# A two-way state scan without its identity matmul: the decayed state copied by ScalarE and added by VectorE, with some steps beside the scan in other places

## The chip, the cores and the metric

The kernel runs on one core of a Trainium2 chip. The metric is the device time of one execution in microseconds. A core has five engines that each work through a queue of their own in order: TensorE (PE in the profile; its weight loads stand apart as PEld), VectorE (DVE), ScalarE (ACT), GpSimd (POOL) and SyncE (SP), which here only issues transfers. They meet at semaphores. An instruction that waits holds up all that stands behind it in its queue.

## What is computed

The reference is a trunk of four layers over 512 latent and 256 context tokens of 1024 channels: a convolution layer, a bidirectional linear-attention layer (RWKV-7), an attention layer and another convolution layer. Only the second one's recurrence matters here. For each of 16 heads of 64 channels, and each of two directions, a 64 x 64 state S is carried over 768 tokens:

```python
def step(S, inp):
    d_t, k_t, v_t, kk_t, a_t = inp[:5]
    sa = jnp.einsum("bhvk,bhk->bhv", S, -kk_t)
    S = (S * d_t[:, :, None, :] + sa[..., None] * (kk_t * a_t)[:, :, None, :]
         + v_t[..., None] * k_t[:, :, None, :])
    out = jnp.einsum("bhvk,bhk->bhv", S, inp[5]) if emit else None
    return S, out
```

## The kernel before

**Tiling.** The recurrence is worked in chunks of 64 tokens, 12 chunks to a sequence. Two heads make a pair that fills the 128 partitions: head 0 on partitions 0 to 63 (`A` in the code), head 1 on 64 to 127 (`B`). There are eight pairs, 0 to 7, and `scan(p, d, G)` carries pair `p` in direction `d` (0 forward, 1 backward) through steps i = 0 to 11. Both directions of a pair are interleaved; the pairs follow each other.

**A step** has six parts, each ended by a `yield`. A tile `VT` holds, for head 0, the state S on rows A and the chunk's values on rows B, and for head 1 the other way round.

1. c: TensorE multiplies `VT` by a triangular matrix `GM` (L1346). For 0 < i < 11 it also multiplies `VT` by a slice of the identity (L1350), which puts S itself into `pS`, as the first term of a sum that is left open.
2. Z: ScalarE copies c from PSUM (L1353).
3. TensorE multiplies S by `AR` into the output `pO` (L1357), and Z by `Tt`, the inverse of a triangular matrix (L1360).
4. U: ScalarE copies the result into `VT` in place of S (L1362, L1363, four copies of 64 x 64 for both directions).
5. TensorE adds the chunk's terms to `pO` (L1366) and `BKT` times `VT` to `pS` (L1369), which closes both sums.
6. S: ScalarE writes the next step's state, `pS` times the chunk's decay `dc`, a scale for each partition (L1374, two copies of 64 x 64 a direction). The output goes from `pO` to the tile `O`, by a ScalarE copy for i in 0, 1, 4, 5, 6, 7 (L1379) and by a VectorE sum in the others (L1381).

`pO` and `pS` are two halves of one PSUM tile `o0` or `o1`.

**What runs beside it.** While pair p is scanned, the same queues prepare later pairs. `feats` makes decays and scaled keys of a quarter (half a sequence of one direction, four to a pair) of a later pair, in eleven steps: step 2 loads and multiplies (L1112, `pz`), step 3 is a tanh on ScalarE (L1116), step 4 a VectorE scaling (L1118, `sg`), step 5 the matmul that sums up decays (L1122, `pc`), step 6 an exponential (L1126, `Dt`), and then GpSimd's products (L1137 to L1144). `grams` builds `GM` and `BKT`. `inverse` computes the 32 x 32 triangular inverses of pair p + 1 in 31 steps of a product and a sum, nearly all on VectorE (L1265, L1268). `values` transposes v on TensorE (L1227) into one PSUM buffer and copies it into `VT`, rows B by VectorE and then rows A by ScalarE (both through `cpy`, L1089 and L1091), four times for half a sequence. `centre` takes the mean off pair p - 1's output and forms its variance.

**What sets the order.** The four compute engines run in the order in which the code records them; there is no scheduler there. A turn of a pair is 72 ticks; the scan does two parts of one direction in a tick, the even ones direction 0 and the odd ones direction 1. After every odd tick those side steps are recorded whose due time lies in the two ticks. The due times are numbers in `OPT`: `D` for the first six steps of `feats` and `F` for the rest (four rows, for the four quarters of a pair, 18 ticks to a quarter), `G` for `grams`, `I` for the inverse, `V0` and `V1` for the nine steps of `values` for the two half sequences. A pair's scan begins at tick 4, so three slots of two ticks repeat: parts 1 and 2 at ticks that leave 4 or 5 when divided by 6 (Z slot), parts 3 and 4 at 0 or 1 (U slot), parts 5 and 6 at 2 or 3 (S slot).

Of the kernel before, what the change touches and what calls it, by code (L numbers as in the profile page):

```python
# [8 lines left out]
F32 = mybir.dt.float32  # L9
F32R = mybir.dt.float32r  # L10
AF = mybir.ActivationFunctionType
ALU = mybir.AluOpType
# [3 lines left out]

D = 1024
P = 128
NT = D // P
CTX = 256  # L20
# [13 lines left out]
    G=[[1.1, 3.6, 4.6, 6.6, 9.6, 11.6, 13.1, 14.6, 17.9], [0.5, 3.1, 5.1, 7.6, 10.6, 11.6, 12.6, 14.6, 17.1], [1.6, 3.6,  # L34
        5.1, 5.1, 8.1, 12.1, 12.1, 14.1, 15.6], [1.6, 3.6, 5.1, 7.6, 9.6, 11.6, 13.1, 15.1, 16.6]],
    F=[[2.65, 6.65, 10.65, 15.65, 16.65], [3.65, 7.15, 9.65, 17.4, 17.9], [3.15, 7.15, 10.65, 16.15, 17.9], [1.65, 7.15, 10.65, 15.65, 17.9]],
    D=[[8.2, 13.7, 13.7, 14.2, 17.4, 17.9], [5.7, 12.7, 14.2, 16.9, 17.9, 17.9], [9.2, 12.7, 13.2, 13.7, 16.7, 17.7],
        [8.2, 13.7, 14.2, 14.7, 17.7, 17.9]],
    L=0.85,
    I=[3.9, 7.5, 8.4, 8.5, 9.75, 9.75, 9.75, 9.9, 11.9, 12.25, 13.5, 13.75, 13.9, 15.25, 15.4, 15.75, 17, 17.15, 17.65,  # L40
# [3 lines left out]
    V0=[31.91, 36.16, 37.91, 39.91, 40.91, 42.41, 43.66, 45.41, 46.91],  # L44
    V1=[47.92, 51.4375, 52.96, 54.43, 55.4275, 57.16, 58.42, 60.415, 62.1869],
    A=[64.18, 65.3143, 66.1364, 69.4498, 69.7397, 70.3889],
    B=[2.44, 4.09473, 7.27024, 8.71365, 9.3943, 9.83957],
    C=[12.2, 14, 16.1, 16.15, 18.75, 20.8, 21.45, 22.9, 23.55, 26.6, 28.95, 29.25, 32.1, 33.4, 36.55, 37.75],
# [30 lines left out]
class Trunk:  # L79
# [111 lines left out]
    def modulation(self, i, w=512):  # L191
# [3 lines left out]
        b = self.vbase[f"mod_b{i}"]  # L195
        half, nq = D // 2 // w, w // P
        order = [x * 2 * half + y for h in range(2) for x in (0, 1) for y in range(h * half, h * half + half)]
# [93 lines left out]
    def conv_layer(self, i, j, lat_only, filler):  # L291
# [27 lines left out]
        parts = {"a": 0, "b": 1, "g": 2}  # L319
        cols = [w_in[:, parts[x] * D + m * P: parts[x] * D + (m + 1) * P] for x, m in order if x != "c"]  # L320
        with tc.tile_pool(name="cv", bufs=1) as cv, tc.tile_pool(name="cd", bufs=1, space=DRAM) as cd:
# [340 lines left out]
    def rwkv_features(self, i, c1, cv):  # L662
# [103 lines left out]
        def modulation(i, w=256):  # L766

            modT, b = self.modT[i], self.vbase[f"mod_b{i}"]
            half, nq = D // 2 // w, w // P
            order = [x * 2 * half + y for h in range(2) for x in (0, 1) for y in range(h * half, h * half + half)]  # L770
# [257 lines left out]
    def rwkv_scan(self, i, rk, cv, vproj):  # L1028
        nc, tc, I = self.nc, self.tc, self.I
        C = 64  # L1030
# [9 lines left out]
        late = {}  # L1040
# [18 lines left out]
        ident = self.ident  # L1059
        self.mask3 = self.mask.rearrange("p (g c) -> p g c", c=C).unsqueeze(1).to_broadcast([P, 3, 2, C])  # L1060
        A, B = slice(0, 64), slice(64, 128)
# [24 lines left out]
        def cpy(key, k, out, in_):  # L1086
            e = OPT["E"][key][k]
            if e == "a":
                nc.scalar.activation(out, in_, AF.Copy)  # L1089
            elif e == "d":  # L1090
                nc.vector.tensor_copy(out, in_)  # L1091
            else:
                nc.gpsimd.tensor_scalar(out=out, in0=in_, scalar1=1.0, scalar2=0.0, op0=ALU.mult, op1=ALU.add)
# [235 lines left out]
        def scan(p, d, G):  # L1329


            if d == 0:
                G["O"] = late["s"].tile([P, TOK], F32, tag="O", name="O", bufs=2)
            O, Tt = G["O"], G["Tt"]
            for i in range(12):
                h, q = divmod(i, NQ)
                assert (p, h) in vdone and (p, h, d) in gdone and (p, h) in idone
                VT, GM, AR, BKT = (G["VT", h], *(G[n, h, d] for n in ("GM", "AR", "BKT")))
                dc = G["DC", h, d][:, q:q + 1]
                hc = lambda hd: slice(hd * C, (hd + 1) * C)  # L1340
                pc = late["c"][d][:, 0:2 * C].rearrange("p (n c) -> p n c", c=C)
                po = late["p"].tile([P, 2 * C], F32, tag=f"o{d}", name=f"o{d}")
                pO, pS = po[:, 0:C], po[:, C:]
                for hd, own, oth in ((0, A, B), (1, B, A)):
                    rows = oth if i == 0 else slice(0, P)
                    nc.tensor.matmul(pc[own, 0, :], GM[rows, 2 * hd, q, :], VT[rows, d, q, hc(hd)], start=True, stop=True)  # L1346

                if 0 < i < 11:
                    for hd, own in ((0, A), (1, B)):
                        nc.tensor.matmul(pS[own], ident[:, hc(hd)], VT[:, d, q, hc(hd)], start=True, stop=False)  # L1350
                yield
                Z = late["s"].tile([P, C], F32, tag=f"Z{d}", name="Z", bufs=1)
                cpy("Z", d, Z, pc[:, 0, :])  # L1353
                yield
                if i:
                    for hd, own in ((0, A), (1, B)):
                        nc.tensor.matmul(pO[own], VT[own, d, q, hc(hd)], AR[own, 1, q, :], start=i == 11, stop=False)  # L1357
                tu = (h * 2 + d) * NQ + q
                for own in (A, B):
                    nc.tensor.matmul(pc[own, 1, :], Tt[own, tu, :], Z[own], start=True, stop=True)  # L1360
                yield
                cpy("U", 2 * d, VT[A, d, q, 0:C], pc[A, 1, :])  # L1362
                cpy("U", 2 * d + 1, VT[B, d, q, C:2 * C], pc[B, 1, :])  # L1363
                yield
                for hd, own in ((0, A), (1, B)):
                    nc.tensor.matmul(pO[own], VT[:, d, q, hc(hd)], GM[:, 2 * hd + 1, q, :], start=i == 0, stop=i == 11)  # L1366
                if i < 11:
                    for hd, own in ((0, A), (1, B)):
                        nc.tensor.matmul(pS[own], BKT[:, q, hc(hd)], VT[:, d, q, hc(hd)], start=False, stop=True)  # L1369
                yield  # L1370
                if i < 11:
                    h2, q2 = divmod(i + 1, NQ)
                    for hd, own in ((0, A), (1, B)):
                        nc.scalar.activation(G["VT", h2][own, d, q2, hc(hd)], pS[own], AF.Copy, scale=dc[own])  # L1374

                c0 = (i if d == 0 else (3 - i if i < 4 else 15 - i)) * C
                oc = O[:, c0:c0 + C] if d == 0 else O[:, c0:c0 + C][:, ::-1]
                if i in (0, 1, 4, 5, 6, 7):
                    cpy("O", d, oc, pO)  # L1379
                else:  # L1380
                    nc.vector.tensor_tensor(out=oc, in0=pO, in1=oc, op=ALU.add)  # L1381
                if i == 11:
                    sdone.add((p, d))
                yield
# [40 lines left out]
        def named(g, label):  # L1425
            while True:
                self.mark(label)
                try:
                    v = next(g)
                except StopIteration:  # L1430
                    return
                yield v
# [9 lines left out]
        def stream():  # L1442

            for n in range(-2, len(quarters)):
                ev = []
                for times, g in ((OPT["G"][n % 4], gg[n:n + 1] if n >= 0 else []), (OPT["F"][n % 4], fg[n + 1:n + 2]),
                                 (OPT["D"][n % 4], fg[n + 2:n + 3])):
                    if g:
# [6 lines left out]
        def side(p):  # L1455
# [5 lines left out]
            def run(g, times):  # L1461
                ev.extend((t, lambda g=g: next(g, None)) for t in times)

            if nxt:
                iv = named(inverse(p + 1, G), f"inverse{p + 1}")
                ev.append((OPT["L"], lambda: load_inverse(p + 1, G)))
                run(iv, OPT["I"])
                run(named(values(p + 1, 0, G), f"values{p + 1}"), OPT["V0"])
                run(named(values(p + 1, 1, G), f"values{p + 1}"), OPT["V1"])
                i64 = G["i64"] = named(inverse64(p + 1, G), f"inverse64{p + 1}")  # L1470
# [7 lines left out]
        with ExitStack() as man:  # L1478
# [11 lines left out]
            for w in range(6):  # L1490
                ev = next(X)
                for n in range(18):
                    v_steps(18 * w + n)
                    for t, g in ev:
                        if n <= t < n + 1:
                            next(g)
            chain = {p: [named(scan(p, d, GS[p]), f"scan{p}") for d in range(2)] for p in range(NT)}
            for p in range(-1, NT + 1):
                ev = side(p)
# [47 lines left out]
            out = named(self.readout(), "L1y")  # L1547
# [542 lines left out]
```

## Time and profile before

| | |
|---|---|
| median of three runs | 2456.02 us (2451.81 to 2461.89) |
| the profiled execution | 2455.47 us |
| its span, first to last instruction | 2453.7 us |
| mean granted TensorE clock | 0.957 |
| the scan: first c product to the last one's start | 869.0 to 1396.9 us |
| ScalarE's scaled copies of S, L1374 | 352, 108.9 us busy, 309 ns each |
| identity products, L1350 (two records to a matmul) | 640 records, 49.1 us busy |
| VectorE's sums of the output, L1381 | 96, 20.1 us busy, 221 ns each |
| VectorE's `sg`, L1118 | 32, 23.8 us busy, median 360, longest 2034 ns |

A row of a group names line, engine, operation, the output and input tiles and their shapes, the count, then busy time and mean duration of one in ns, and after a second bar the idle time ahead of these instructions and who ended it. A row of the timeline has start and length in us, then the same names; brackets hold the idle time of its engine just before. A row of waits has the total in us, the number of times and the longest. A row of windows has the length of the window and for each engine the busy time and the number of instructions, then the granted clock, the share of the DMA engines and GB/s.

### The profile page before, as it was taken

The page shows a single profiled execution, that of the slowest core. Times are in us where ns is not written, and L with a number is a line of the kernel's source. Part 1 is how long each engine was busy: PE and PEld are TensorE (multiplying, and loading weights), DVE is VectorE, ACT ScalarE, POOL GpSimd, SP SyncE. Part 2 cuts the span into 40 slices and gives each one's busy share as a digit, 9 for nine tenths or more (in the row PEclk, how much of TensorE's full clock was granted, in tenths as well). Part 3 has the DMA queues.
Part 4 walks back from the last instruction along what each step waited for, and adds up shares of the span by engine and source line. Part 5 has one row for each costly group of instructions (what it writes and reads, how often), then busy time and mean ns, then how long its engine had stood idle before and what let it go on. Part 6 is the DMA issues. An engine that isn't in the chain of part 4 may idle for free. (4 is left out here: it accounts for less than half of the span.)

```text
span 2453.7 us, 45772 instructions
## 1 busy us (share of the span) xinstructions
PE 2237.2 (91%) x17983; PEld 1771.9 (72%) x17983; DVE 1413.5 (58%) x2565; ACT 1103.7 (45%) x2642; POOL 511.3 (21%) x600
## 2 busy tenths in 40 slices
PE   7999979799988788888888999888999999989987
PEld 4677757576666667777766678888999889865655
DVE  3866565734463767666664243556455464667774
ACT  4321233315552266666667543455455454432232
POOL 0000001000111232232210014544454454410000
PEclk8999989999999899999988999999999999989999
DMA  8776633275756654445434481111111121304442
GB/s 274 218 226 198 197 106 122 65 234 172 210 176 202 170 126 119 111 121 124 120 75 129 132 239 46 53 35 52 52 52 52 56 66 52 95 22 132 126 127 80
DMA packets 358998, 304.50 MB, mean 124 GB/s; under 512 B 110887, under 2 KB 300415, under 8 KB 358783
## 3 DMA queue, kind: packets, MB, share of 16 engines
q1 hardware_dynamic: 358782, 301.57, 42.5%
q8 instruction: 142, 2.33, 0.4%
q14 instruction: 74, 0.60, 0.1%
HBM read 215.82 MB, written 57.77 MB: 112 GB/s over the span
## 5 line engine op out<-in xcount | busy, mean ns | idle before, releaser
L173 ACT ACTIVATE whi<-wraw 128x1024 fp32r<-128x1024 f32 x168 | 177.0, 1056 | 373.7 <-PE cps L186 180.8
L175 DVE TENSOR_TENSOR wlo<-wraw,whi 128x1024 fp32r<-128x1024 f32 x98 | 120.4, 1229 | 169.2 <-ACT whi L173 167.6
L175 POOL TENSOR_TENSOR wlo<-wraw,whi 128x1024 fp32r<-128x1024 f32 x70 | 168.6, 2412 | 185.4 <-ACT whi L173 171.1
L370 DVE SCALAR_TENSOR_TENSOR Y<-yp,VC,Y 128x783 f32<-128x783 f32 (+1 forms) x224 | 196.8, 891 | 8.1 <-ACT Y L363 4.2
L1843 PE MATMUL pj<-whi,hhi 128*128 128x256 f32 x640 | 182.0, 285 | 5.5 <-ACT junk L1852 3.9
L186 PE MATMUL cps<-hhi,whi 128*128 128x512 f32 x576 | 179.0, 367 | 3.3 <-ACT hhi L285 3.3
L1843 PE MATMUL pj<-wlo,hhi 128*128 128x256 f32 x640 | 181.3, 284 | 0.0
L1843 PE MATMUL pj<-whi,hlo 128*128 128x256 f32 x640 | 181.1, 284 | 0.0
L186 PE MATMUL cps<-hhi,wlo 128*128 128x512 f32 (+1 forms) x576 | 177.0, 361 | 0.0
L186 PE MATMUL cps<-hlo,whi 128*128 128x512 f32 (+1 forms) x576 | 176.6, 360 | 0.0
L186 PEld LDWEIGHTS cps<-hhi,whi 128*128 128x128 f32 x576 | 96.6, 190 | 48.0 <-issue 16.7
L186 PE MATMUL ops<-hhi,whi 128*128 128x512 f32 (+1 forms) x320 | 104.5, 368 | 25.7 <-ACT hhi L445 23.4
L1843 PEld LDWEIGHTS pj<-whi,hhi 128*128 128x128 f32 x640 | 123.0, 192 | 6.8 <-ACT junk L1852 4.5
L1843 PEld LDWEIGHTS pj<-wlo,hhi 128*128 128x128 f32 x640 | 123.0, 192 | 0.7
L1843 PEld LDWEIGHTS pj<-whi,hlo 128*128 128x128 f32 x640 | 122.7, 192 | 0.1
L1374 ACT ACTIVATE VT<-o,DC 64x64 f32<-64x64 f32 x352 | 108.9, 309 | 27.5 <-PE o L1369 18.1
L186 PEld LDWEIGHTS cps<-hhi,wlo 128*128 128x128 f32 x576 | 95.9, 189 | 25.8 <-issue 10.0
L186 PEld LDWEIGHTS cps<-hlo,whi 128*128 128x128 f32 x576 | 96.7, 190 | 22.7 <-issue 5.0
L1089 ACT ACTIVATE VT<-c 64x64 f32<-64x64 f32 x384 | 83.8, 218 | 54.7 <-PE c L1360 46.4
L186 PE MATMUL ops<-hhi,wlo 128*128 128x512 f32 (+1 forms) x320 | 105.7, 360 | 3.0 <-POOL wlo L175 2.2
L186 PE MATMUL ops<-hlo,whi 128*128 128x512 f32 (+1 forms) x320 | 104.3, 354 | 0.0
L1268 DVE TENSOR_TENSOR Ti<-Ti,tm 96x31 f32<-96x31 f32 (+15 forms) x248 | 99.7, 402 | 7.3 <-POOL tm L1265 1.3
(347 smaller groups left out, 5685.4 us busy)
## 6 DMA issues: line engine op xcount, KB each, us to landing
mraw<-in_mod_w_dram SPq DMA_DIRECT2D x36, 1024.0 KB
wraw<-in_conv_w_in_dram SPq DMA_DIRECT2D x48, 512.0 KB
wraw<-in_attn_w_in_dram SPq DMA_DIRECT2D x48, 512.0 KB
X<-yp SPq DMA_DIRECT2D x128, 99.4 KB
mraw<-in_mod_w_dram SPq DMA_DIRECT2D x24, 512.0 KB
KR<-dF SPq DMA_DIRECT2D x24, 384.0 KB
F<-dF SPq DMA_DIRECT2D x24, 384.0 KB
X<-yp SPq DMA_DIRECT2D x128, 65.5 KB
```

Of the source, the lines that this page charges most:

```text
L173: nc.scalar.activation(hi[:, :n], raw[:, :n], AF.Copy)
L175: lo_eng.tensor_tensor(out=lo[:, :n], in0=raw[:, :n], in1=hi.bitcast(F32)[:, :n], op=ALU.subtract)
L186: nc.tensor.matmul(ps, a[:, k, m0:m0 + m], b[k0 + k][:, ts], start=first and k == 0 and i == 0, stop=last and k == kt - 1 and i == 2)
L370: taps.append(lambda v=v: nc.vector.scalar_tensor_tensor(out=Y[m], in0=y[:, PE_TAPS + v:PE_TAPS + v + nout], scalar=self.vec("dw", nv)[:, ...
L1089: nc.scalar.activation(out, in_, AF.Copy)
L1268: eng("ia", j).tensor_tensor(out=Ti[0:96, j + 1:32, 0:c], in0=Ti[0:96, j + 1:32, 0:c], in1=o, op=ALU.add)
L1374: nc.scalar.activation(G["VT", h2][own, d, q2, hc(hd)], pS[own], AF.Copy, scale=dc[own])
L1843: nc.tensor.matmul(o[:, n, :], a, b[:, k, :], start=kh == 0 and k == 0 and e == 0 and n == 0, stop=kh == 1 and k == 3 and e == 2 and n == 1)
```

## The change

The identity product is gone. In the Z slot, right after a direction's Z copy, ScalarE now makes `SD`, S times the decay, from `VT`, before U overwrites S. In the S slot VectorE forms the new state as `pS` times the decay plus `SD`, with one instruction for each head (new line L1377). At i = 0, where there is no state yet, ScalarE still scales `pS`, and at i = 11 no state is formed. The new lines shift those behind them by one to five.

```diff
     G=[[1.1, 3.6, 4.6, 6.6, 9.6, 11.6, 13.1, 14.6, 17.9], ...
-    D=[[8.2, 13.7, 13.7, 14.2, 17.4, 17.9], [5.7, 12.7, 14.2, 16.9, 17.9, 17.9], [9.2, 12.7, 13.2, 13.7, 16.7, 17.7],
-        [8.2, 13.7, 14.2, 14.7, 17.7, 17.9]],
+    D=[[8.2, 12.1, 12.6, 13.9, 17.4, 17.9], [5.7, 12.7, 13.2, 13.9, 17.9, 17.9], [9.2, 12.7, 13.2, 13.7, 16.7, 17.7],
+        [8.2, 12.1, 12.6, 13.7, 17.7, 17.9]],
...
-    V0=[31.91, 36.16, 37.91, 39.91, 40.91, 42.41, 43.66, 45.41, 46.91],
+    V0=[31.91, 35.5, 35.9, 38.5, 38.9, 42.4, 43.66, 45.41, 46.91],
...
-                if 0 < i < 11:
-                    for hd, own in ((0, A), (1, B)):
-                        nc.tensor.matmul(pS[own], ident[:, hc(hd)], VT[:, d, q, hc(hd)], start=True, stop=False)
                 yield
                 Z = late["s"].tile([P, C], F32, tag=f"Z{d}", name="Z", bufs=1)
                 cpy("Z", d, Z, pc[:, 0, :])
+
+                if 0 < i < 11:
+                    SD = late["s"].tile([P, C], F32, tag=f"SD{d}", name="SD", bufs=1)
+                    for hd, own in ((0, A), (1, B)):
+                        nc.scalar.activation(SD[own], VT[own, d, q, hc(hd)], AF.Copy, scale=dc[own])
                 yield
                 if i:
                     for hd, own in ((0, A), (1, B)):
-                        nc.tensor.matmul(pO[own], VT[own, d, q, hc(hd)], AR[own, 1, q, :], start=i == 11, stop=False)
+                        nc.tensor.matmul(pO[own], VT[own, d, q, hc(hd)], AR[own, 1, q, :], start=True, stop=False)
...
                     for hd, own in ((0, A), (1, B)):
-                        nc.scalar.activation(G["VT", h2][own, d, q2, hc(hd)], pS[own], AF.Copy, scale=dc[own])
+                        S = G["VT", h2][own, d, q2, hc(hd)]
+                        if i:
+                            nc.vector.scalar_tensor_tensor(out=S, in0=pS[own], scalar=dc[own], in1=SD[own], op0=ALU.mult, op1=ALU.add)
+                        else:
+                            nc.scalar.activation(S, pS[own], AF.Copy, scale=dc[own])
```

The due times move `sg` (step 4 of `feats`) of three of the four quarters from the S slot or the next Z slot into the U slot, and with it the tanh and the matmuls ahead of it to the front of their slot or a slot earlier. Of `values`, the first transposes and copies move from the U into the Z slot, and the second ones into the S slot; `V1` is changed in the same manner.

The first place is VectorE's queue around the second `sg` of a pair's turn, step i = 4 of the scan, in a middle pair. Before:

```order
L1166 TENSOR_TENSOR GM<-pg,C 128x3x2x64 x2
L1268 TENSOR_TENSOR Ti<-Ti,tm 96x14x18
L1265 TENSOR_TENSOR tm<-inst,Ti 96x247
L1268 TENSOR_TENSOR Ti<-Ti,tm 96x13x19
L1265 TENSOR_TENSOR tm<-inst,Ti 96x240
L1268 TENSOR_TENSOR Ti<-Ti,tm 96x12x20
L1118 TENSOR_SCALAR sg<-sg 128x384
L1265 TENSOR_TENSOR tm<-inst,Ti 96x231
```

Now:

```order
L1166 TENSOR_TENSOR GM<-pg,C 128x3x2x64 x2
L1268 TENSOR_TENSOR Ti<-Ti,tm 96x14x18
L1265 TENSOR_TENSOR tm<-inst,Ti 96x247
L1118 TENSOR_SCALAR sg<-sg 128x384
L1377 SCALAR_TENSOR_TENSOR VT<-o_10635,DC,SD 64x64 x2
L1377 SCALAR_TENSOR_TENSOR VT<-o_10643,DC,SD 64x64 x2
L1268 TENSOR_TENSOR Ti<-Ti,tm 96x13x19
L1265 TENSOR_TENSOR tm<-inst,Ti 96x240
L1268 TENSOR_TENSOR Ti<-Ti,tm 96x12x20
L1265 TENSOR_TENSOR tm<-inst,Ti 96x231
L1091 COPY VT<-pv 64x4x64
```

`sg` stands three instructions earlier, and the four new sums of the state (two heads in each of two directions) stand right behind it, in the middle of the inverse (L1265, L1268).

The second place is ScalarE's queue in the next step, i = 5, from the Z copies to the S slot; `c_6724` and `c_6725` are the c tiles of the two directions. Before:

```order
L1089 ACTIVATE Z<-c_6724 128x64
L1089 ACTIVATE Z<-c_6725 128x64
L1089 ACTIVATE BKT<-pt 128x384
L1126 ACTIVATE Dt<-pc 128x6x64
L1089 ACTIVATE VT<-c_6724 64x64 x2
L1089 ACTIVATE VT<-c_6725 64x64 x2
L1089 ACTIVATE VT<-pv 64x3x64
L1374 ACTIVATE VT<-o_12762,DC 64x64 x2
L1089 ACTIVATE O<-o_12762 128x64
L1374 ACTIVATE VT<-o_12769,DC 64x64 x2
L1089 ACTIVATE O<-o_12769 128x64
```

Now:

```order
L1089 ACTIVATE Z<-c_6724 128x64
L1354 ACTIVATE SD<-VT,DC 64x64 x2
L1089 ACTIVATE Z<-c_6725 128x64
L1354 ACTIVATE SD<-VT,DC 64x64 x2
L1089 ACTIVATE BKT<-pt 128x384
L1089 ACTIVATE VT<-pv 64x3x64
L1126 ACTIVATE Dt<-pc 128x6x64
L1089 ACTIVATE VT<-c_6724 64x64 x2
L1089 ACTIVATE VT<-c_6725 64x64 x2
L1089 ACTIVATE O<-o_12871 128x64
L1089 ACTIVATE O<-o_12879 128x64
```

The scaled copies have left the S slot, SD stands between and behind the Z copies, and the copy of v (`VT<-pv`) has moved from behind the U copies (`VT<-c`) to ahead of them.

The third place is VectorE's queue in step i = 10, around the last `sg` of the turn. Before:

```order
L1091 COPY TP<-px 32x384 x2
L1166 TENSOR_TENSOR GM<-pg,C 128x3x2x64
L1381 TENSOR_TENSOR O<-o_11081,O 128x64
L1381 TENSOR_TENSOR O<-o_11088,O 128x64
L1118 TENSOR_SCALAR sg<-sg 128x384
```

Now:

```order
L1091 COPY TP<-px 32x384 x2
L1166 TENSOR_TENSOR GM<-pg,C 128x3x2x64
L1118 TENSOR_SCALAR sg<-sg 128x384
L1377 SCALAR_TENSOR_TENSOR VT<-o_11159,DC,SD 64x64 x2
L1386 TENSOR_TENSOR O<-o_11159,O 128x64
L1377 SCALAR_TENSOR_TENSOR VT<-o_11167,DC,SD 64x64 x2
L1386 TENSOR_TENSOR O<-o_11167,O 128x64
```

Here `sg` has moved from behind the output sums to ahead of the new sums.

More of the change, by code (lines that the diff above doesn't have):

```diff
@@ L43 @@
         40.9, 41.65, 42.15, 44.25, 44.9, 45.9, 46.25, 46.65, 47.25, 47.65, 48.9],
-    V0=[31.91, 36.16, 37.91, 39.91, 40.91, 42.41, 43.66, 45.41, 46.91],
-    V1=[47.92, 51.4375, 52.96, 54.43, 55.4275, 57.16, 58.42, 60.415, 62.1869],
+    V0=[31.91, 35.5, 35.9, 38.5, 38.9, 42.4, 43.66, 45.41, 46.91],
+    V1=[47.92, 51.4, 51.9, 54.4, 55.4, 58.4, 58.9, 61.5, 62.2],
     A=[64.18, 65.3143, 66.1364, 69.4498, 69.7397, 70.3889],
```

## The prediction

> **What bounds the kernel now.** Times are of the profiled execution: 2455.47 us, of which the span is 2453.7; the median of the three timed runs, 2456.02, is 0.02% above it, so the sum is made against 2455.5. I first read the share of the engines on the page, then the scan alone.
>
> ```profile
> PE 2237.2 (91%) x17983; PEld 1771.9 (72%) x17983; DVE 1413.5 (58%) x2565; ACT 1103.7 (45%) x2642; POOL 511.3 (21%) x600
> ```
>
> By this line PE bounds everything and work taken off it should pay. The change touches the scan only, so the windows decide; here is one turn of the scan (the tile pair from one `sg` step to the same step of the next pair), cut in two. The first window is the half in which VectorE works through the 31 steps of the next pair's inverse; I call it half A, the other half B.
>
> ```profile
> core 0: us, PE busy (x) PEld busy (x) DVE busy (x) ACT busy (x) POOL busy (x), PEclk, DMA share, GB/s
> 1078.04:1112.04 34.00, 29.61 (x399) 22.43 (x397) 29.77 (x74) 22.90 (x88) 9.10 (x12) 1.00 0.37 102
> 1112.04:1144.10 32.06, 28.97 (x554) 24.40 (x552) 16.67 (x43) 22.22 (x81) 10.30 (x14) 0.95 0.62 137
> ```
>
> In A, VectorE is busy for 29.77 of 34.00 us, as much as PE. In B it is half idle. The 4.23 us that it has left in A are the number on which all hangs. Part of them are the small gaps between dependent instructions; the waits that the timeline names in A are four:
>
> ```profile
> 1080.90 0.42 DVE L1399 SCALAR_TENSOR_TENSOR O<-gm,O 128x256 f32<-128x256 f32 x1 [0.81 <-PE gm L1396]
> 1096.44 1.26 DVE L1118 TENSOR_SCALAR sg<-sg 128x384 f32<-128x384 f32 x1 [1.08 <-ACT sg L1116]
> 1100.70 1.92 DVE L1268 TENSOR_TENSOR Ti<-Ti,tm 96x192 f32<-96x192 f32 x1 [0.16 <-POOL tm L1265]
> 1112.04 0.36 DVE L1118 TENSOR_SCALAR sg<-sg 128x384 f32<-128x384 f32 x1 [0.73 <-ACT sg L1116]
> ```
>
> They sum to 2.78 us. PE waits as follows, in five turns (935 to 1265 us):
>
> ```profile
> PE pc L1122 <- DVE sg L1118: 13.4, 9, 2.1
> PE pv L1227 <- ACT VT L1089: 8.2, 10, 1.4
> ACT VT L1089 <- DVE VT L1091: 20.3, 20, 1.4
> ```
>
> The first two are 2.7 and 1.6 us a turn, and the moved steps aim at both. The third says who is behind the second: ScalarE's copy of v waits for VectorE's copy into the same tile.
>
> **The change part by part.** A step of the scan has three slots: c and Z; U; then the products into o, with the new state S.
>
> *Identity products out.* PE's timeline of one step:
>
> ```profile
> 1085.21 0.29 PE L1346 MATMUL c<-VT,GM 128*64 128x64 f32 x4
> 1085.33 0.29 PE L1350 MATMUL o<-VT,C 128*64 128x64 f32 x4
> 1085.54 0.70 PE L1396 MATMUL gm<-O,C 128*128 128x256 f32 x2
> ```
>
> The identity pair of one direction takes 0.12 us from start to start and the second 0.2, so about 0.3 us for both directions; ten steps of a turn make 3 us at most. Where PE waits for the state anyway, this gives nothing.
>
> *ScalarE.* It loses 20 pairs of scaled copies in a turn and gains 20 pairs of SD copies of the same 64x64 shape, also with a scale from memory.
>
> ```profile
> 1078.03 0.64 ACT L1374 ACTIVATE VT<-o,DC 64x64 f32<-64x64 f32 x2
> 1078.70 0.22 ACT L1089 ACTIVATE O<-o 128x64 f32<-128x64 f32 x1
> 1078.95 0.64 ACT L1374 ACTIVATE VT<-o,DC 64x64 f32<-64x64 f32 x2
> ```
>
> A pair is 0.64 us, and I take the same for SD, so the engine's sum stays. The place changes: SD of the first direction stands between the two Z copies, so the second Z and all U copies come up to 0.64 and 1.28 us later; the S slot is emptied of 1.28. What queues behind SD is Z, U, and with U PE's products into o. As the U copies of half A in any case find PE or VectorE late, I charge this only in B.
>
> *VectorE's new instruction.* In a step four of them, 64x64 from PSUM, with a scalar from memory. No row shows that shape, so it is bounded:
>
> ```profile
> L1381 DVE TENSOR_TENSOR O<-o,O 128x64 f32<-128x64 f32 x96 | 20.1, 221 | 66.9 <-ACT VT L1374 30.0 <-PE o L1366 23.0 <-PE pt L1188 5.5
> L461 DVE SCALAR_TENSOR_TENSOR xc<-ops,modT,xc 128x256 f32<-128x256 f32 x8 | 3.7, 466 | 3.3 <-PE ops L186 3.3
> L1399 DVE SCALAR_TENSOR_TENSOR O<-gm,O 128x256 f32<-128x256 f32 x24 | 10.1, 419 | 18.5 <-PE gm L1396 18.5
> ```
>
> The 64-column sum from PSUM is 221 ns; a scalar from memory adds 466 - 419 = 47; so about 0.27 us each. How densely they stand is the question, and two places of the timeline answer it differently:
>
> ```profile
> 1089.83 0.34 DVE L1381 TENSOR_TENSOR O<-o,O 128x64 f32<-128x64 f32 x2
> 1090.10 0.41 DVE L1265 TENSOR_TENSOR tm<-inst,Ti 96x256 f32<-96x256 f32 x1
> ```
>
> ```profile
> 1104.10 0.30 DVE L1265 TENSOR_TENSOR tm<-inst,Ti 96x135 f32<-96x135 f32 x1
> 1104.43 0.29 DVE L1091 COPY VT<-pv 64x128 f32<-64x128 f32 x1
> 1104.76 0.36 DVE L1091 COPY V<-Vr 128x384 f32<-128x384 f32 x1
> ```
>
> Two O sums on all 128 partitions overlap: 0.27 us for both, 0.13 each. The copy into the lower half of VT starts 0.03 us after the end of what is ahead of it, and so does what follows it. The new instructions write the upper and the lower half in turn, like that copy, so I take 0.27 + 0.03 = **0.30 us each**, with 0.13 as the lower end and the 0.33 of ScalarE's alternating pair as the upper.
>
> The Trainium skill ("VectorE: DVE Perf Modes", section "Two Vector instructions with no wait between them") has a rule for this: an instruction whose operand or output starts in another group of 32 partitions than the last one's is held until all earlier ones have finished. By it every second new instruction, and the one behind it, gets no overlap; without it the sum below would be 24 x 0.13 and A would not grow. The trace agrees with it in the rows above.
>
> *Half A.* Between the first and the fourth `sg` of a turn stand 12 pairs, 24 new instructions: 24 x 0.30 = 7.2 us (3.1 to 7.9). One centring step L1399 (0.42 in the row above), ahead of the first `sg` before, falls behind it. Against this: the 2.78 of named waits can be filled, and the second `sg`, 1.26 us beside a GpSimd product, goes ahead of that product (first row below): 0.36 as in the last of the four rows, 0.90 less. Sum 7.2 + 0.42 - 2.78 - 0.90 = **+3.9 us** on A (-0.2 to +4.6). VectorE's queue sets the step here, since the state now comes from it: between the sums of two steps stand five to ten products of the inverse (0.41 the long ones), in order, and PE's c products wait for the sums, Z and U behind them. What PE saved turns into waits for `VT <- DVE`. The moved `sg` does remove the 1.34 us below, and the earlier copies of v the 1.41 (first and second of the PE rows), but both waits lie in A, where VectorE's sum decides, so I count neither. The copies of v now stand ahead of U on ScalarE and behind inverse work on VectorE, whose copy they wait for: a new wait of up to 2 us that A's sum also covers.
>
> ```profile
> 1096.44 0.99 POOL L1144 TENSOR_TENSOR BK<-F,iD 128x384 f32<-128x384 f32 x1
> ```
>
> ```profile
> 1097.76 0.94 PE L1122 MATMUL pc<-C,sg 128*128 128x128 f32 x6 [1.34 <-DVE sg L1118]
> 1105.26 0.63 PE L1227 MATMUL pv<-C,V 128*128 128x128 f32 x4 [1.41 <-ACT VT L1089]
> 1130.31 1.02 PE L1122 MATMUL pc<-C,sg 128*128 128x128 f32 x6 [2.12 <-DVE sg L1118]
> ```
>
> *Half B.* The last row's 2.12 us go: this `sg` moves into the U slot, ahead of GpSimd's products, and PE's next matmuls find it done. Identity: four steps, some 0.2 us each that are not hidden, 0.8. Cost: in four steps SD ahead of Z and U, up to 1.28 us, of which the emptied S slot gives back about 1: 0.3 each, 1.2; the O copies of one step on ScalarE wait for the new sums, which read the same tile, 0.3; ScalarE's copy of v ahead of U waits for VectorE's, 20.3 / 20 = 1.0 in the row above, 0.8 of it new. Sum -2.1 - 0.8 + 1.2 + 0.3 + 0.8 = **-0.6 us** (-3, if the costs hide, to +2, if nothing of the S slot comes back).
>
> *The scan.* +3.3 us a turn, in six turns (pairs 0 to 5): +20. Pair 6 has the inverse but no `sg`: +3. In pair 7 VectorE is idle and PE is full of the gate stream: SD costs and the identity saves, 0. Ahead of the scan the moved `sg` and v copies give -1. Sum +22: **2455.5 + 22 = 2478 us**, +0.9%; with the ends of both halves, -3.2 and +6.6 a turn, 2438 to 2497.
>
> **The rivals.** (1) *Faster: VectorE has room.* 4.23 us over 24 instructions is 0.176 us each: below that A does not grow and the waits removed count. Then A gives -1.34 - 1.41 and B about -1.9: -4.6 a turn, six turns, -28: 2428 us. For it: O sums at 0.13. Against: the held copies above, and the named waits of 2.78 make the point 0.12 rather than 0.176. (2) *No change:* the instructions cost about 0.2 and PE's gain pays for A's growth: 2455, within 10. (3) *Slower still: the sums collide with GpSimd.* GpSimd is busy for 19.4 us of the two halves, 29%, and some VectorE instructions wait for it:
>
> ```profile
> L1118 DVE TENSOR_SCALAR sg<-sg x32: 349/360/2034, 756.6 to 1227.5; 128x384 f32<-128x384 f32 x32
> L1381 DVE TENSOR_TENSOR O<-o,O x96: 208/224/226, 886.4 to 1400.0; 128x64 f32<-128x64 f32 x96
> ```
>
> `sg` goes from 349 to 2034 ns, SBUF to SBUF. If each of the 40 sums of a turn that meets GpSimd lost half of one of its 0.99 us products, it would be 40 x 0.29 x 0.5 = 5.8 us a turn, six turns, +35 on top of the forecast: 2512. Against it: the O sum, with one operand from PSUM like the new instruction, never exceeds 226. The Trainium skill ("SBUF — State Buffer", section "SBUF: two separate sides") limits that lock to VectorE instructions with two SBUF inputs or in a two-port mode, which spares the new one; the second row agrees. (4) *Slower by ScalarE:* SD ahead of U costs 0.6 in each of ten steps, 6 us a turn in A too, +48 over eight turns: 2503. Against it: ScalarE is busy for 22.90 of 34 us in A.
>
> **How the numbers follow.** A measurement of this kernel tells some 0.5%, 12 us, from no change. Chances: the forecast 0.50 (0.07 of it below 2468), (1) 0.17, (2) 0.20, (3) 0.08, (4) 0.05. So faster 0.17, same 0.27, slower 0.56. The range leaves out most of (1) and the end of (3): 2432 to 2512.
>
> **What would show it.** Right: in the windows of A, VectorE's busy time near 37 us of 38; the longest wait of PE's c products is for VT from VectorE; L1122 no longer waits for `sg`; the new line's busy time is 320 x 0.27 = 86 us, and spaced 0.30. Wrong: pairs of new instructions that take 0.4 us together, A still near 34 us with VectorE gaps in it, or a new line whose slowest instruction is over 1 us.

## The result, and the profile after

The changed kernel took **2523.41 us** (median of 4 runs, 2521.57 to 2525.85) against 2455.75 for the kernel before (4 runs): a ratio of 1.0264, 95% interval 1.0243 to 1.0284, 67.7 us slower. The forecast was 2478, with a range up to 2512. The direction was right, the forecast growth of 22 us was a third of the measured one.

The page's line of the engines shows how little a share says here: the 320 identity products (640 records) are gone from PE, and yet it has more busy time than the 2237.2 us of before. The products that are left take longer in the mean; the last section comes back to that.

```profile
PE 2259.5 (90%) x17343; PEld 1782.6 (71%) x17343; DVE 1488.9 (59%) x2885; ACT 1118.8 (44%) x2642; POOL 509.5 (20%) x600
```

These are the windows of the changed kernel that answer to halves A and B, between the same `sg` steps of a turn (columns as in the prediction):

```profile
1104.84:1145.54 40.70, 32.32 (x363) 24.47 (x358) 36.69 (x99) 24.30 (x87) 9.25 (x12) 0.92 0.31 87
1145.54:1178.72 33.18, 28.70 (x510) 23.60 (x512) 17.96 (x57) 22.57 (x79) 10.13 (x14) 0.95 0.59 132
```

Half A grew from 34.00 to 40.70 us. VectorE is busy for 36.69 of it, close to the 37 of the forecast. But the forecast had nearly filled VectorE's idle time there, and 4.01 us of it are left, as against 4.23 before. The 2.78 us of named waits were to be filled; two waits are left in A, 1.77 us in all:

```profile
1125.09 0.36 DVE L1118 TENSOR_SCALAR sg<-sg 128x384 f32<-128x384 f32 x1 [0.69 <-ACT sg L1116]
1145.54 0.36 DVE L1118 TENSOR_SCALAR sg<-sg 128x384 f32<-128x384 f32 x1 [1.08 <-ACT sg L1116]
```

Who PE waits for shows a second cause. First the waits of the kernel before, in five turns (935 to 1265 us); the columns are the sum in us, the times and the longest:

```profile
PEld o L1366 <- ACT VT L1089: 9.6, 39, 1.1
PEld c L1360 <- ACT Z L1089: 4.8, 10, 0.6
PE c L1360 <- ACT Z L1089: 3.4, 10, 0.4
PE o L1366 <- ACT VT L1089: 2.1, 6, 1.0
```

Now those of the changed kernel over some five turns (944 to 1307 us; L1361 and L1367 are the lines L1360 and L1366 of before):

```profile
PEld o L1367 <- ACT VT L1089: 32.5, 50, 1.6
PEld c L1361 <- ACT Z L1089: 28.3, 35, 1.9
PE o L1367 <- ACT VT L1089: 23.7, 31, 1.4
PE c L1361 <- ACT Z L1089: 23.4, 34, 1.8
PEld c L1346 <- DVE VT L1377: 10.3, 23, 1.4
PE c L1346 <- DVE VT L1377: 4.2, 5, 0.9
```

The wait for VectorE's new sums, which the prediction put first, is the smallest of these. (That alone does not clear VectorE: e3 below finds its queue to be the limit in half A.) PE waits for **ScalarE**, for Z and for U: 3.4 + 2.1 became 23.4 + 23.7, some 8 us a turn. One step on ScalarE shows what happened. Before (the tenth step of a turn):

```profile
1118.94 0.46 ACT L1089 ACTIVATE Z<-c 128x64 f32<-128x64 f32 x2 [0.35 <-PE c L1346]
1119.34 0.32 ACT L1089 ACTIVATE VT<-pv 64x192 f32<-64x192 f32 x1
1119.72 0.95 ACT L1089 ACTIVATE VT<-c 64x64 f32<-64x64 f32 x4
1120.76 1.31 ACT L1374 ACTIVATE VT<-o,DC 64x64 f32<-64x64 f32 x4
```

And the same step of the changed kernel, ScalarE and then VectorE:

```profile
1154.31 0.22 ACT L1089 ACTIVATE Z<-c 128x64 f32<-128x64 f32 x1 [2.09 <-PE c L1346]
1154.56 0.72 ACT L1354 ACTIVATE SD<-VT,DC 64x64 f32<-64x64 f32 x2
1155.30 0.22 ACT L1089 ACTIVATE Z<-c 128x64 f32<-128x64 f32 x1
1155.55 0.71 ACT L1354 ACTIVATE SD<-VT,DC 64x64 f32<-64x64 f32 x2
1156.29 0.32 ACT L1089 ACTIVATE VT<-pv 64x192 f32<-64x192 f32 x1
1156.52 0.93 ACT L1089 ACTIVATE VT<-c 64x64 f32<-64x64 f32 x4
```

```profile
1157.71 0.60 DVE L1377 SCALAR_TENSOR_TENSOR VT<-o,DC,SD 64x64 f32<-64x64 f32 x2 [0.90 <-PE o L1367]
1158.34 0.23 DVE L1386 TENSOR_TENSOR O<-o,O 128x64 f32<-128x64 f32 x1
1158.48 0.59 DVE L1377 SCALAR_TENSOR_TENSOR VT<-o,DC,SD 64x64 f32<-64x64 f32 x2
```

From the first Z to the first U it was 0.78 us, and it is 2.21: 1.43 more, the two SD pairs. What ScalarE no longer does at the end of this step gives it nothing back, because VectorE's four sums, with an O sum between them, take from 1157.71 to 1159.07, 1.36 us, as long as ScalarE's four copies (1.31). The step has become longer by a serial piece, on an engine that is busy for 68% of this half (22.57 of 33.18 us).

### The profile page after: what moved, and what is told of

It reads as the page before. It is cut to its first block, busy times and chain, and to the rows that moved or that the text cites. A ratio compares the mean times of both kernels' runs of the same rounds, so it can differ in the third digit from the quotient of the medians.

```text
span 2522.0 us, 44859 instructions
## 1 busy us (share of the span) xinstructions
PE 2259.5 (90%) x17343; PEld 1782.6 (71%) x17343; DVE 1488.9 (59%) x2885; ACT 1118.8 (44%) x2642; POOL 509.5 (20%) x600
## 5 line engine op out<-in xcount | busy, mean ns | idle before, releaser
L186 PE MATMUL ops<-hhi,whi 128*128 128x512 f32 (+1 forms) x320 | 104.5, 368 | 27.0 <-ACT hhi L445 23.4
L1367 PE MATMUL o<-GM,VT 128*64 128x64 f32 x768 | 90.1, 261 | 36.7 <-ACT VT L1089 36.1
L1377 DVE SCALAR_TENSOR_TENSOR VT<-o,DC,SD 64x64 f32<-64x64 f32 x320 | 90.1, 282 | 40.5 <-PE o L1370 25.9
L1354 ACT ACTIVATE SD<-VT,DC 64x64 f32<-64x64 f32 x320 | 110.3, 345 | 7.7
L1367 PEld LDWEIGHTS o<-GM,VT 128*64 128x64 f32 x768 | 65.8, 150 | 62.3 <-ACT VT L1089 52.8
```

The lines of the kernel that those rows point to most:

```text
L186: nc.tensor.matmul(ps, a[:, k, m0:m0 + m], b[k0 + k][:, ts], start=first and k == 0 and i == 0, stop=last and k == kt - 1 and i == 2)
L1354: nc.scalar.activation(SD[own], VT[own, d, q, hc(hd)], AF.Copy, scale=dc[own])
L1377: nc.vector.scalar_tensor_tensor(out=S, in0=pS[own], scalar=dc[own], in1=SD[own], op0=ALU.mult, op1=ALU.add)
```

## The experiments

Two causes stood against each other: *theory 1*, SD on ScalarE; *theory 2*, the recorded one, VectorE full in half A; and as a third the moved steps. Ratios and differences are to the kernel before in the same set of runs. That kernel's median went from 2455.75 to 2462.75 us between the sets, so where two variants of different sets are compared, two figures stand: the difference of their medians and that of their distances from the kernel before.

**e1: the moved steps alone.** The three lists `D`, `V0`, `V1` of the change, in the kernel before.

> The kernel before with the identity products and ScalarE's state copies kept; only the new due times of the decays' steps and of the copies of v are taken over. Theory 1 (the decayed copy SD on ScalarE stands ahead of Z and U and lengthens nearly every step; the moved steps are a small matter): 2440 to 2465 us. Theory 2 (the recorded forecast: VectorE is the bound in half A through its 24 new sums): the sums are not here, so 2440 to 2460. Theory 3 (the moved steps are what costs, by copies of v that stand ahead of U): 2490 or more.

2460.39 against 2461.34 us, ratio 1.0004 (0.9988 to 1.0020): no change.

**e2: the changed kernel with the old lists.**

> The changed kernel with the due times of before: only the identity products, the SD copies and the sums differ from before. Theory 1: 2510 to 2530 us, since all SD copies are there. Theory 2: also over 2500, with VectorE near 37 us busy of 38 in half A. Theory 3: 2480 or less.

2546.22 us, ratio 1.0342 (1.0316 to 1.0368), 17 to 23 us above the changed kernel. Theory 3 falls; theory 2's "over 2500" holds, theory 1's range was too low. All three missed that the moved steps *help* here.

**e3: without SD.** The old state is left out of the new one.

```
-                if 0 < i < 11:
-                    SD = ...
-                        nc.scalar.activation(SD[own], VT[own, d, q, hc(hd)], AF.Copy, scale=dc[own])
...
-    ... in0=pS[own], scalar=dc[own], in1=SD[own], ...
+    ... in0=pS[own], scalar=dc[own], in1=ident[own, hc(hd)], ...
```

> The changed kernel without the 320 SD copies: the sum on VectorE stays as it is, of the same shape, and adds columns of the identity matrix in place of the decayed state, so the old state is left out. Theory 1: in the trace of the changed kernel Z of the first direction to U takes 7.6 to 9.6 us a turn more than before over ten steps; without SD this goes: 8 turns times 9 = 70, so 2453 us, between 2435 and 2465. Theory 2: VectorE's instructions are all there, so half A stays as long: 2500 to 2525.

2502.56 us, ratio 1.0166 (1.0143 to 1.0190). Theory 1 alone falls: only 21 to 26 of the 67.7 us went, 41 stayed. VectorE's timeline in half A of this run shows what stayed, and behind it PE's row for the products that need the new state:

```profile
1099.10 0.98 DVE L1265 TENSOR_TENSOR tm<-inst,Ti 96x207 f32<-96x207 f32 x1
1100.12 0.96 DVE L1268 TENSOR_TENSOR Ti<-Ti,tm 96x207 f32<-96x207 f32 x1
1101.11 0.38 DVE L1265 TENSOR_TENSOR tm<-inst,Ti 96x220 f32<-96x220 f32 x1
1101.53 0.38 DVE L1268 TENSOR_TENSOR Ti<-Ti,tm 96x220 f32<-96x220 f32 x1
1101.95 0.40 DVE L1265 TENSOR_TENSOR tm<-inst,Ti 96x231 f32<-96x231 f32 x1
1102.26 0.59 DVE L1372 SCALAR_TENSOR_TENSOR VT<-o,DC,C 64x64 f32<-64x64 f32 x2
1102.89 0.23 DVE L1381 TENSOR_TENSOR O<-o,O 128x64 f32<-128x64 f32 x1
1103.03 0.59 DVE L1372 SCALAR_TENSOR_TENSOR VT<-o,DC,C 64x64 f32<-64x64 f32 x2
```

```profile
1102.59 1.41 PE L1346 MATMUL c<-VT,GM 128*64 128x64 f32 x8 [1.15 <-DVE VT L1372]
```

VectorE has no gap and no wait: the sums come when the inverse's products ahead of them are done, and PE waits 1.15 us for them. That is the mechanism of the forecast. Both causes are there, then, and the question became how they share.

**e4: one SD copy in place of two.** Both columns of the state tile are scaled at once, on all partitions.

```
-                    for hd, own in ((0, A), (1, B)):
-                        nc.scalar.activation(SD[own], VT[own, d, q, hc(hd)], AF.Copy, scale=dc[own])
+                    nc.scalar.activation(SD, VT[:, d, q, :], AF.Copy, scale=dc)
```

> The changed kernel with one SD copy of 128x128 a direction in place of two of 64x64 (both columns of the state tile are scaled; the half that no sum reads is waste). Theory 1: a pair holds ScalarE for 0.73 us (0.345 x 2 and the gap); one copy should take 0.40 to 0.45, so 0.3 less ahead of the second Z and 0.3 less ahead of U: 40 per cent of the 70 us come back, 2495 us, between 2480 and 2508. Theory 2: no change, 2515 to 2525.

2508.01 us, ratio 1.0182 (1.0152 to 1.0212). One copy of 128x128 takes 0.395 us where the pair held the engine for 0.72; and as it overlaps its neighbours, the second Z starts only 0.29 us after it (1121.39 to 1121.68 in this run's timeline). That leaves some 5 us above e3 of the 21 to 26 that SD costs. The expectation had sized the share on 70.

**e5: S by VectorE, identity kept.** In the kernel before, only ScalarE's scaled copy of the state goes to VectorE, as one operation.

```
-  nc.scalar.activation(S, pS[own], AF.Copy, scale=dc[own])
+  nc.vector.tensor_scalar(out=S, in0=pS[own], scalar1=dc[own], scalar2=None, op0=ALU.mult)
```

> The kernel before, identity products and all due times kept; only the scaled copy of the new state (320 of 352) goes from ScalarE to VectorE, as one operation from PSUM of about the duration of the sum (0.28 us). It has VectorE's load and the place of the sum in its queue, but no SD copies. Theory A (VectorE is full in half A, the queue makes the sums late, some 6 us a turn): 2490 to 2525 us, like the run without SD (2503) with PE's identity work on top. Theory B (the loss of the run without SD is not VectorE's load but something else in the changed kernel, the missing identity products or the moved steps): 2445 to 2475.

2485.03 against 2459.07 us, ratio 1.0107 (1.0085 to 1.0129): 26 us, less than theory A gave and clear of theory B. VectorE's new load alone makes the kernel slower, with ScalarE relieved and PE's work unchanged.

**e6: SD that nobody reads.** The SD copies added to the kernel before.

> The kernel before with the 320 SD copies added on ScalarE at their new place, read by nobody; identity, ScalarE's state copies and due times kept. It shows what SD costs where VectorE has no new load. If SD ahead of Z and U is worth only the 20 us between the run without SD and the changed kernel: 2470 to 2490. If it is worth the 0.96 us a step that Z to U grew by (77 us over 80 steps) and is half hidden in the changed kernel because VectorE is late there anyway: 2510 to 2540.

2527.04 us, ratio 1.0301 (1.0254 to 1.0347): 68 us. Where VectorE has no new load and ScalarE keeps its own copies of the state, SD costs as much as the whole change.

The windows show the two causes apart. The first stretch of each kernel runs from the first c product of a turn's third step to that of its eighth (the core of half A), the second from there to the third step of the next turn. Kernel before:

```profile
1078.50:1108.03 29.53, 25.15 (x338) 18.85 (x337) 26.20 (x64) 19.34 (x74) 9.10 (x12) 1.00 0.34 96
1108.03:1144.08 36.05, 32.95 (x610) 27.67 (x609) 19.77 (x51) 25.32 (x94) 10.30 (x14) 0.95 0.61 140
```

Changed kernel:

```profile
1105.61:1141.44 35.83, 27.99 (x297) 21.00 (x296) 33.07 (x89) 20.90 (x75) 9.25 (x12) 0.90 0.28 79
1141.44:1179.49 38.05, 33.03 (x569) 27.07 (x569) 21.58 (x66) 25.97 (x91) 10.13 (x14) 0.96 0.59 136
```

S by VectorE (e5):

```profile
1090.45:1125.17 34.72, 29.32 (x337) 21.87 (x336) 31.09 (x85) 13.70 (x54) 9.53 (x12) 0.85 0.30 81
1125.17:1160.22 35.05, 32.29 (x609) 26.72 (x608) 22.93 (x71) 18.92 (x73) 10.30 (x14) 1.00 0.62 145
```

Unread SD (e6):

```profile
1095.42:1126.98 31.56, 25.47 (x337) 18.95 (x336) 25.70 (x64) 26.32 (x94) 9.40 (x12) 1.00 0.32 88
1126.98:1167.63 40.65, 34.57 (x610) 28.40 (x609) 20.11 (x51) 32.45 (x114) 10.27 (x14) 0.96 0.56 126
```

VectorE's load lengthens the first stretch by 5.2 us and shortens the second by 1.0; unread SD weighs the other way round, 2.0 and 4.6. The changed kernel has 6.3 and 2.0. The sums lie behind the inverse in the first stretch. SD costs mostly in the second, and less in the changed kernel than here; e12 takes that up.

**e7 and e8: less inverse.** In the kernel before and in the changed one.

```
-                eng("ia", j).tensor_tensor(...)
+                (j % 2 == 0) and eng("ia", j).tensor_tensor(...)
```

> The kernel before with 15 of the 31 additions of each inverse left out (the odd ones), which takes some 6 us a turn from VectorE in half A. Control for the next: before is not bound by VectorE, so at most the small waits for it go: 2435 to 2460 us.

> The changed kernel with the same 15 additions of each inverse left out. Theory A with both causes adding up (VectorE's load in half A some 40 us, SD on ScalarE some 20): 2475 to 2490 us. If the two hide each other and SD alone carries most: 2500 to 2520. If VectorE's load in half A plays no part: 2515 to 2525.

2448.47 us (ratio 0.9952, 0.9929 to 0.9974) and 2492.44 us (1.0142, 1.0119 to 1.0164). The same relief of VectorE is worth 11 us before and 31 to 34 after: the changed kernel is bound by VectorE there, before was only brushed by it. 2492.44 lies just over the range for two causes that add, and under the one for two that hide each other.

**e9: identity out, nothing in its place.**

> The kernel before without the identity products and with nothing in their place: ScalarE's scaled copy is kept, the old state is left out of the new one. It gives the most that taking 640 products off PE can bring. The recorded working: 3 us a turn at most, 24 us in eight turns, and 0.8 a turn in half B alone. If PE's work bounds the scan: 2430 to 2437 us. If PE mostly waits for the state there: 2445 to 2460. If the missing products are what makes the run without SD (2503) slower than the one with S by VectorE and identity (2485): 2465 to 2475.

2471.41 against 2459.29 us, ratio 1.0036 (1.0015 to 1.0058). PE without the 320 products is not faster, 12 us slower if anything, which is the third case of the expectation. But of the 17 us that its profiled execution is longer than that of the kernel before, 10 lie behind the start of the scan's last step, where the two kernels do nearly the same, and 4 in the first six turns. Where they come from stays open.

**e10: e5 with the new lists.**

> The run with S by VectorE, identity kept (2485 us), with the new due times of the decays' steps and copies of v added; nothing left out. It splits the 17 us between that run and the one without SD (2503). If the moved steps cost when VectorE is full: about 2503. If they help, as they do between the sums with the old due times (2546) and the changed kernel (2523): 2462 to 2478. If they do nothing, as without the sums: 2480 to 2490, and the 17 us belong to the sum's form or the missing identity.

2498.78 us, ratio 1.0142 (1.0117 to 1.0166), 14 us above e5, which is most of the 17 between e5 and e3. So the moved steps are worth 0 in the kernel before, +14 with S by VectorE and -17 to -23 with the sums and SD (e2). Their effect has no size of its own; why the signs differ was not taken apart.

**e11: SD by VectorE.**

> The changed kernel with the SD copies made by VectorE, same shapes, nothing left out. ScalarE's load goes, VectorE gets 320 more instructions of some 0.15 to 0.28 us, 24 of them in half A of each turn, where it is full. If both causes are as found: the run without SD (2503) plus 24 times 0.15 to 0.28 in seven turns, 25 to 47: 2528 to 2550 us. If ScalarE alone matters: 2503 or less.

2556.72 us, ratio 1.0379 (1.0352 to 1.0406), 7 us over the expected range. Besides the load in half A, some of the copies met a GpSimd product. The new instructions of this run in the view of one tile (ns least, median, most), and then one such place in the timeline:

```profile
L1354 DVE TENSOR_SCALAR SD<-VT,DC x320: 236/254/1503, 882.0 to 1476.1; 64x64 f32<-64x64 f32 x160
L1377 DVE SCALAR_TENSOR_TENSOR VT<-o,DC,SD x320: 266/284/292, 885.7 to 1482.1; 64x64 f32<-64x64 f32 x160
```

```profile
1089.26 1.00 POOL L1144 TENSOR_TENSOR BK<-F,iD 128x384 f32<-128x384 f32 x1
1089.47 1.12 DVE L1354 TENSOR_SCALAR SD<-VT,DC 64x64 f32<-64x64 f32 x2
```

**e12: no SD and less inverse.** The edits of e3 and e7 together.

> The run without SD (identity columns added in place of the old state) with the 15 odd additions of each inverse left out as well. Fourth corner of the square: all additions with and without SD 2523 and 2503, 16 of 31 additions with SD 2492, before with 16 of 31 2448. If VectorE's load in half A and SD on ScalarE are the whole loss: 2440 to 2458 us. If a third cause is left: over 2465.

2459.17 us, ratio 0.9993 (0.9978 to 1.0008), between the two ranges of the expectation. With both causes taken away, 2523 falls to 2459, some 11 us above the light kernel before (e7). By the medians SD costs 21 us with the full inverse and 33 with the light one, which looks as if the two causes hid each other. The traces say otherwise. These are the first six turns of the scan (first c product of pair 0 to that of pair 6, in one profiled execution each), where all side work is there:

| six turns, us | full inverse | light inverse |
|---|---|---|
| kernel before | 391.6 | 381.2 (e7) |
| changed kernel without SD | 419.1 (e3) | 385.3 (e12) |
| changed kernel | 439.0 | 403.9 (e8) |

SD costs 20 us in one column and 19 in the other; the inverse's weight costs 34 us without SD and 35 with it. In these turns the two simply add, and with both taken away the changed kernel is 4 us above the light kernel before. The 12 us between 21 and 33 lie outside these turns, in pairs 6 and 7 and ahead of and behind the scan. What the change costs without SD falls from 27.5 us to 4 with the lighter inverse.

The same turns show why SD costs less than in e6. There it adds 44 us, 13 in the first stretches and 31 in the second ones; in the changed kernel it adds 6 and 14 over e3, so less than half in either. In e6 ScalarE keeps its copies in the S slot, in the changed kernel they are gone. That fits a slot that gives back about half, but the identity and the due times differ between the two kernels as well, so it is not shown apart.

**e13: SD earlier.** e4 with the copy in the slot ahead of Z, where ScalarE waits for c.

```
+                if 0 < i < 11:
+                    SD = ...
+                    nc.scalar.activation(SD, VT[:, d, q, :], AF.Copy, scale=dc)
                 yield
                 Z = late["s"].tile([P, C], F32, tag=f"Z{d}", name="Z", bufs=1)
```

> The run with one SD copy a direction (0.395 us each, 2508 us), with the copy issued one slot earlier: both directions' copies stand ahead of both Z copies, where ScalarE waits for PE's c products for some 0.45 us and more. If it is SD's place between Z and U that costs, the wait for c hides the first copy and most of the second: 2503 us, as without SD, or less. If any ScalarE time between the state and U costs the same: 2505 to 2512. If SD holds the first Z and with it everything behind it: over 2515.

2510.54 us, ratio 1.0202 (1.0168 to 1.0235), as e4: the place between the state and U made no difference that these runs can tell, of the some 5 us that SD costs in this form. U overwrites the state, so SD must stand somewhere in that stretch.

**e14 and e15: the decays' steps alone, and the copies of v alone,** in the kernel before (5 rounds).

> The kernel before with only the due times of the decays' steps changed. The run with all moved steps was 1.5 us a turn shorter than before in five turns and 4 us longer ahead of the scan. If both the gain and the loss are the decays' (their wait for sg goes, 2.1 us a turn in half B): 2445 to 2455 us if the loss ahead is the copies' of v, 2455 to 2463 if it is theirs too.

> The kernel before with only the due times of the copies of v changed. If the copies bring the gain in the turns: 2445 to 2455 us. If they only move waits from PE to ScalarE's queue (ScalarE's wait for VectorE's copy grew from 20 to 31 us in five turns with all steps moved): 2458 to 2470.

2447.80 against 2462.75 us, ratio 0.9935 (0.9914 to 0.9956), and 2482.81 us, 1.0092 (1.0062 to 1.0122), the first as expected, the second over both ranges. The two nearly cancel in e1. **The list `D` alone makes a kernel that is faster than both**, by 15 us than the one before. PE no longer waits for `sg`, so ScalarE gets the decays' product `pc` at once; before, and in e14 (both 935 to 1265 us):

```profile
PE pc L1122 <- DVE sg L1118: 13.4, 9, 2.1
ACT Dt L1126 <- PE pc L1122: 13.4, 18, 2.0
```

```profile
ACT Dt L1126 <- PE pc L1122: 2.4, 9, 0.3
```

In e14 there is no row left of PE waiting for `sg`.

## Why the prediction was right or wrong

**The bound.** Right. VectorE sets half A as soon as the state comes from it (e5, and the 31 us or more of e8 against 11 of e7). The growth there was put at 24 instructions of 0.30 us less 2.78 us of waits, 4.4 before the moved steps; e5 shows 5.2 in its first stretch of five steps, 4.6 in the mean of six turns. Of the signs, VectorE's busy time in A is as forecast (36.69 us, but of 40.70 and not of 38), and L1122 has no row of waiting for `sg` in the five turns above. The sign for PE fails: its long waits are for Z and U.

**VectorE's new instruction.** Right in size and in spacing. Estimated 0.27 us, spaced 0.30, 86 us in all; it measured 90.1 us, and the changed kernel has these rows for the new lines:

```profile
L1377 DVE SCALAR_TENSOR_TENSOR VT<-o,DC,SD x320: 267/284/293, 884.1 to 1459.5; 64x64 f32<-64x64 f32 x160
L1354 ACT ACTIVATE SD<-VT,DC x320: 335/344/351, 880.6 to 1454.6; 64x64 f32<-64x64 f32 x160
```

In e3's timeline above, the lower half's sum never overlaps the upper's (0.59 us for two), while the sum of the upper half after an O sum starts 0.14 us after it. The Trainium skill ("VectorE: DVE Perf Modes", section "Two Vector instructions with no wait between them") holds back an instruction that starts in another group of 32 partitions than the one ahead; the trace agrees. No sum exceeds 0.293 us, so rival 3, GpSimd's lock on the sums, is out.

**SD on ScalarE: the step that failed.** "As the U copies of half A in any case find PE or VectorE late, I charge this only in B", and there at 0.3 a step, because "the emptied S slot gives back about 1". That made 1.2 us a turn, 7 us in six turns. The traces have 20 us in these turns (changed kernel over e3), and the medians 21 to 26 us for the whole kernel. Both grounds failed. Of the 13 us missing, 6 lie in the first stretches, where SD was put at nothing, and 7 in the second ones (14.3 us, or some 0.5 a step and not 0.3; they hold five of the ten steps with SD, half B four). An SD pair also takes 0.72 us and not 0.64. And that the emptied slot gives little back has a reason in the timelines above: VectorE takes as long for that link of the chain (1.36 us) as ScalarE did (1.31), so only ScalarE's other work can gain. The range, too, was too narrow here: "if nothing of the S slot comes back" makes the sum of half B +3.3 by its own terms, where it is given as +2; the end would be 2505 and not 2497.

**Rival 4** was this very mechanism, at 0.6 in each of ten steps, and had a chance of 0.05, on the ground that ScalarE is busy for 22.90 of 34 us. A share of busy time cannot speak against a delay in a serial chain. Its 48 us were about twice the 21 to 26 measured. And it was held to *exclude* the forecast, while the two add: mostly VectorE in the first stretch, mostly ScalarE in the second.

**Identity.** 0.8 us a turn expected, that is 5 us; e9 shows none. Why the kernel without these products is not faster stays open.

**The moved steps.** The decays were put at +0.42 - 0.90 - 2.1 a turn, 15 us in six turns, and e14's median is 15 lower. That the numbers meet is partly luck: in the traces the second stretches of e14 are 2.5 us a turn shorter, near the 2.1, but the first ones are 0.5 longer, six turns make 12.6 us, and the scan starts 4.3 us later. The copies of v were put at 0.8 a turn in B, 5 us; alone they cost 20, and 2.75 a turn of it in the second stretches against 0.1 in the first. So the wait in A cost nothing to speak of, and the term in B was more than three times too small. "Ahead of the scan the moved `sg` and v copies give -1" was wrong too: the first c product starts at 874.2 instead of 869.0 us, 5 us later, and in e14 at 873.3, so most of it is the decays'.

**The sum.** Half A: +3.9 forecast, +6.7 by the windows between `sg` steps; half B: -0.6 forecast, +1.6 (33.18 against 31.57 from 1112.04 to the `sg` at 1143.61). In six turns that was to be +20 and is +47.4. SD is 13 of the 27 us missing. The rest shows in e3, which has no SD: its first stretches are 5.0 a turn longer than before, where A was put at +3.9, and its second ones 0.3 shorter, where B without SD was put at 1.8 shorter (the identity's 0.8 did not come, the copies of v cost more). Outside the six turns the forecast had +2 and the profiled executions have +21: pair 6 grew by 9.6 us and not 3, pair 7 by 2.1 and not 0, the part ahead by 5.2, and 4 us lie behind the start of the last step, where no SD and no new sum stands.

## What to carry to other kernels

In a loop whose steps depend on each other, follow one value round the step and add up every engine's piece on its way; an instruction put into that way can cost up to its full length however idle its engine is on average (unread SD, 1.43 us a step, cost 44 of 86 us in six turns), and moving a link to another engine saves only the difference of the two links. Before calling two slow mechanisms rivals, ask whether they sit in different stretches of time, for then they can add, as here. And take a change that bundles schedule and arithmetic apart: here one of three lists was a gain that the rest buried.

## What the runs showed of the hardware

ScalarE, too, does not overlap the copies here that alternate between partition halves: the 0.344 us SD copies come 0.37 apart and the four U copies of 0.22 take 0.93, while two 128-partition copies (the Z of a step without SD, below) take 0.34. No run tells the alternation apart from the smaller number of partitions.

```profile
1169.86 0.34 ACT L1089 ACTIVATE Z<-c 128x64 f32<-128x64 f32 x2 [1.10 <-PE c L1346]
```

So one copy of 128x128 (0.395 us), with four times the elements of one of 64x64, beat two of those (0.72).

GpSimd delayed VectorE's SD copies from SBUF to SBUF (e11: median 0.254, most 1.503 us) but not the sums, which read PSUM and one operand from SBUF (most 0.292). The Trainium skill ("SBUF — State Buffer", section "SBUF: two separate sides") has a lock of that kind for instructions with two SBUF inputs or in a two-port mode; the SD copy has one tensor input, so it would be the latter; no run shows the mode.

The granted clock fell with the change, from 0.957 to 0.940 in the mean and from 0.96 to 0.91 in the six turns, and the same products on PE took longer: L1162, which the change does not touch, before and after (mean 309 and 331 ns):

```profile
L1162 PE MATMUL pg<-AR,BK 64*128 64x128 f32 x768 | 67.2, 309 | 2.3 <-DVE BK L1144 1.5 <-POOL Dt L1125 0.4 <-DVE GM L1166 0.4
```

```profile
L1162 PE MATMUL pg<-AR,BK 64*128 64x128 f32 x768 | 74.2, 331 | 2.6 <-DVE BK L1144 1.5 <-DVE GM L1166 1.1
```

The median does not show it (272 ns in both). PE's busy time in the six turns rose from 346.6 to 361.9 us, with the identity products gone. The clock there goes from 0.87 (e11) to 0.98 (e1, e12) over the runs, but not by PE's busy share: in the windows above it is 0.85 at 84% (e5, first stretch) and 1.00 at 81% (e6). How much of the 67.7 us comes this way, and whether the clock fell because PE waited more, no run tells. A lower clock is thus a third part of the loss that is neither excluded nor measured.
